# A hybrid Fourier and neighbourhood-attention block on one core: the two passes over the MLP's weights are parted, one put beside the queries, one beside the values, and the context's norm is made in steps

## The chip, the core and the metric

One core of a Trainium2 chip runs the whole program: TensorE (PE in the profile; PEld is its weight load), VectorE (DVE), ScalarE (ACT), GpSimd (POOL), SyncE (SP, which here only issues transfers) and 16 DMA engines. The metric is the device time of one execution in microseconds, the lower the better.

## What is computed

One layer, one batch, 2048 latent tokens of 1024 channels and 256 context tokens. What matters for the change, cut from the reference:

```
sh1, sc1, g1, sh2, sc2, g2 = ada_mod(c, w_ada, b_ada)       # silu(c) @ w_ada + b_ada, six times 1024
csh1, csc1, ...            = ada_mod(c_ctx, w_ada, b_ada)
hc = modulate(rms_norm(ctx, norm1_g), csh1, csc1)           # context: only keys and values are used
fc, qc, kc, vc = split_projection(hc @ w_in)
hx = modulate(rms_norm(x, norm1_g), sh1, sc1)
fx, qx, kx, vx = split_projection(hx @ w_in)                # 4 x 512 columns
...
gates = sigmoid(hx @ w_branch_gate)                         # 2048 columns
...
x   = x + g1 * mixed
hx2 = modulate(rms_norm(x, norm2_g), sh2, sc2)
x   = x + g2 * (relu(hx2 @ w_mlp1) ** 2) @ w_mlp2
```

## The kernel before, in words

The program is one stream of Python calls that a scheduler orders engine by engine; at run time every engine works through its own list in that order, and an instruction whose operand is missing holds what stands behind it on its engine. SP issues nearly all transfers, and its list too is in order: a load that waits for its buffer holds every store behind it.

**Input stage.** `run_pair(n)` goes through eight pairs of 256-column weight units (`seq`, line 689): two Fourier units; two gate units; a query unit with a gate unit (twice); two value units; a key unit with a gate unit (twice); two gate units. Matrix products are three float16 products (high and low halves, `mm3`, line 76), into four PSUM tiles of 2 KB per partition (`mmp`, 4 buffers) that all kinds of units share. A gate or Fourier unit makes 128 channels x 512 tokens with 24 matmuls of 512 columns, which ACT evicts (`put_T`, line 516, tile `ot`, 2 buffers) and SP stores. A query or key unit makes 128 tokens x 256 columns with 24 matmuls of 256 columns: ACT squares it (`sq`, line 572), DVE sums and scales, POOL takes the power (`rstd_from`, line 171), DVE normalises (`qn`, 577), turns (585 to 588), and three units later PE transposes the result (`tq`, 603), and ACT and DVE split it (`sH`, `sL`). A value unit is evicted by ACT (`vo`, line 646, 2 buffers), DVE takes its largest value (648), SP stores it.

I name the pairs by their place: the **gates** (pair 1), the **first queries** and the **second queries** (pairs 2 and 3, each 16 query units and 8 gate units), the **values** (pair 4: 36 units, context's four among them).

**Side work.** Beside the units runs a generator, `side_work` (line 294). `tick` (line 440) moves it on after each unit: three steps per two units in the gates, one per unit in the queries and values. Its steps, in order: context's shift and scale (`c`: eight parts of two steps; a part is a load of 1 MB of `w_ada` into tile `awt`, 2 buffers, and a weighted sum on DVE, `ada_sum`, lines 274 to 277); the second norm's shift and scale (`m`, eight parts); the two residual gains (`g`, eight parts of two steps, with a small bias load `br`); the bias table of the attention (`wm`: three steps, each a load, a subtraction on POOL and a store to `tT`; lines 325 to 327); then 32 steps `w12m`, each a load of 1 MB of an MLP weight into the same two `awt` buffers. For the 16 parts of `w_mlp1` DVE takes the largest magnitude (line 338), for the 16 of `w_mlp2` ACT sums the squares (line 340). From both come the scales `msc`, with which the MLP's weights are then prepared (`early_blocks`, tiles `raw`, `wo`, `ws`), from the end of the side work on.

**Context's norm.** At the start of pair 3 the two context tiles are loaded and normalised (`load_x`), and `build` (line 223) makes the normalised, modulated, transposed and split `hc` in one go: for each of eight channel groups two transposes on PE (`tp_c`, line 229), a scale and shift on ACT or DVE in turn (`ht_c`, 235 or 233), the high half on ACT (236), the low half on DVE (237). `hc` is first used by the value units of context.

Of the kernel before, what the change touches and what calls it, by code (L numbers as in the profile page):

```python
# [8 lines left out]
F32 = mybir.dt.float32  # L9
F32R = mybir.dt.float32r  # L10
F16 = mybir.dt.float16
# [10 lines left out]
C = 256  # L22
# [41 lines left out]
def dit_block(ctx: ExitStack, tc: tile.TileContext, a, out, taps=None, upto=9):  # L64
# [125 lines left out]
    def load_x(src, r0, name, xh=None, sq_on_dve=False, scale_on_dve=False):  # L190
        if xh is None:
            xh = pb.tile([128, D], F32, tag="xh", name=f"xh_{name}", bufs=5)
        load(xh, src[r0:r0 + 128, :])
        sq = pb.tile([128, D], F32, tag="xsq", name=f"xsq_{name}")
        ss = pb.tile([128, 1], F32, tag="ss", name=f"ss_{name}", bufs=4)
        if sq_on_dve:
            dve.tensor_tensor_reduce(out=sq, in0=xh, in1=xh, op0=ALU.mult, op1=ALU.add, scale=1.0, scalar=0.0, accum_out=ss)
        else:
            act.activation(sq, xh, AF.Square, accum_out=ss)
        rs = rstd_from(pb, ss, 1, 1.0 / D, name)  # L200
        if scale_on_dve:
            dve.tensor_scalar(out=xh, in0=xh, scalar1=rs, scalar2=None, op0=ALU.mult)
        else:
            act.activation(xh, xh, AF.Copy, scale=rs)
        return xh
# [17 lines left out]
    def build(hx, xhs, ab, name):  # L223

        w = hx.shape[3]
        for k in range(KT):
            tp = tpp.tile([128, 512], F32, tag="tp", name=f"tp_{name}_{k}")[:, :w]
            for i, xh in enumerate(xhs):
                pe.transpose(tp[:, i * 128:(i + 1) * 128], xh[:, k * 128:(k + 1) * 128], ident)
            sc, bi = ab[:, 8 + k:9 + k], ab[:, k:k + 1]  # L230
            t = pb.tile([128, 512], F32, tag="ht", name=f"ht_{name}_{k}", bufs=2)[:, :w]
            if k % 2:
                dve.tensor_scalar(out=t, in0=tp, scalar1=sc, scalar2=bi, op0=ALU.mult, op1=ALU.add)
            else:
                act.activation(t, tp, AF.Identity, bias=bi, scale=sc)
            act.activation(hx[:, 0, k], t, AF.Copy)
            dve.tensor_tensor(out=hx[:, 1, k], in0=t, in1=hx[:, 0, k], op=ALU.subtract)
        return hx

    def power_of_two(dst, top, floor):  # L240

# [38 lines left out]
    def ada_cols(dst, j, c0, gain, name, acc, wt=None, nk=KT):  # L280

        ps = adp.tile([128, 512], F32, tag="ad", name=f"ad{name}")
        for i in range(2):
            bs = slice(i * 128, (i + 1) * 128)

            for k in range(nk, KT):
# [4 lines left out]
        dve.scalar_tensor_tensor(out=dst[:, 8 + j:9 + j], in0=dst[:, 8 + j:9 + j], scalar=1.0, in1=gain,  # L291
                                 op0=ALU.add, op1=ALU.mult)

    def side_work():
        for dst, d0, s0, g0, o in ((ABc, 0, 8, 16, "c"), (AB2, 3 * D, 0, 24, "m")):
            for k in range(KT):
                c0 = d0 + k * 128
                acc = ada_sum(ada_load(c0, c0 + D, f"{o}{k}"), s0, f"{o}{k}")
                yield
                ada_cols(dst, k, c0, vecT[:, g0 + k:g0 + k + 1], f"{o}{k}", acc)  # L300
                yield
            if o == "c":
                norm_scale(ABc, 1, "c")
                yield
# [17 lines left out]
        for ct in range(3):  # L322
# [3 lines left out]
            pool.tensor_tensor(t, t, view(r, 63 + (0, -8, -8)[ct], [[-1, 16], [1, w]]), op=ALU.subtract)  # L326
            sp.dma_start(tT[ct].rearrange("c d k -> d c k"), t)
            yield
        for i in range(32):
            wt = pb.tile([128, KT, 256], F32, tag="awt", name=f"w12m{i}", bufs=2).rearrange("p k n -> p (k n)")  # L330
            j = i % 16
            if i < 16:
                sp.dma_start(wt, a["w_mlp1"][0, j // 2 * 128:(j // 2 + 1) * 128, j % 2 * 2048:(j % 2 + 1) * 2048])
            else:
                sp.dma_start(wt.rearrange("p (k n) -> p k n", k=2),
                             a["w_mlp2"][0, j * 256:(j + 1) * 256, :].rearrange("(k p) n -> p k n", p=128))
            if i < 16:
                dve.tensor_reduce(out=w1m[:, j:j + 1], in_=wt, axis=AX.X, op=ALU.max, apply_absolute_value=True)
            else:
                act.activation(wt, wt, AF.Square, accum_out=w2m[:, j:j + 1])  # L340
            yield
        m = pb.tile([128, 10], F32, tag="msd", name="msd")
        for i, src in enumerate((w1m, AB2[:, 8:16], w2m, AB2[:, 0:8])):
            dve.tensor_reduce(out=m[:, i:i + 1], in_=src, axis=AX.X, op=ALU.max, apply_absolute_value=True)
# [542 lines left out]
    for n in range(len(seq)):  # L887
        if n == 1:
            with tc.issue_after(last_load[0].ins):
                load_gains()  # L890
                load_rope()
        if n == 3:
            xh_c = [load_x(a["ctx"][0], i * 128, f"c{i}") for i in range(2)]
            hx["c"] = build(pb.tile([128, 2, KT, C], F16, tag="hc", name="hc"), xh_c, ABc, "c")
        if n == len(seq) - 1:
            for o in beside + blocks[:1]:
                for _ in o:
                    pass
            turn(0)
            adp.release()  # L900
            tpp.release()
            pb.release()
            fb = sbuf("ffb")
            chp = psum("ffch", 3)
            smp = psum("ffsm", 1)
            chan = fb.tile([128, 392], F32, tag="chan", name="chan")
            sp.dma_start(chan, a["chan"])
            beside = [fourier_prep()]
        run_pair(n)
        if seq[n][0][0] == "v":  # L910
            beside.append(split_values())
# [952 lines left out]
```

## Time and profile before

| | us |
|---|---|
| median of three runs (lowest, highest) | 2658.93 (2656.83, 2659.85) |
| the profiled execution's own time | 2660.88 |
| its span, first to last instruction | 2659.1 |
| PE busy in the span | 2538.6 (95%) |
| DVE, ACT, POOL busy | 1827.3 (69%), 1183.3 (44%), 484.4 (18%) |
| mean granted TensorE clock | 0.985 |

The span is the time from the first to the last instruction on the core; 1.8 us of the execution's time lie around it. PE is busy through nearly all of it, so what PE loses is read stage by stage: its idle time, what it waited for, and how fast its matmuls ran just after. The gates run from 157 to 244 us, the first queries to 335, the second queries to 449, the values to 556.

### The profile page before, as it was taken

How to read it: one execution, taken by the hardware profiler on the slowest of the kernel's cores; microseconds unless marked ns; L12 is line 12 of the kernel's file. 1: busy time of each engine (PE TensorE's matmuls, PEld its weight loads, DVE VectorE, ACT ScalarE, POOL GpSimd, SP SyncE). 2: the span in 40 equal slices, each digit the busy share in tenths (PEclk: the TensorE clock that was granted, in tenths of full speed). 3: DMA queues.
4: the chain of work that ended last, by engine and by line, in shares of the span. 5: the costliest groups of instructions: out<-in, count | busy, mean ns of one | idle time of the engine just before them, and what ended most of it. 6: DMA issues, size and time to landing. Idle time of an engine off the chain costs nothing.

```text
span 2659.1 us, 42665 instructions
## 1 busy us (share of the span) xinstructions
PE 2538.6 (95%) x15830; PEld 1473.0 (55%) x15830; DVE 1827.3 (69%) x3672; ACT 1183.3 (44%) x2113; POOL 484.4 (18%) x715
## 2 busy tenths in 40 slices
PE   6899989898999899998999999999999999999999
PEld 5445756776656678875666444444444444444444
DVE  6756976568553678887777696978877644636367
ACT  5623225545242577874444564627351333314050
POOL 1201221012224545452000121121211100000000
PEclk9999999999999999998999999999999999999999
DMA  8577689867374744556767777787766533333334
GB/s 269 137 225 204 203 248 304 270 204 245 93 249 141 199 118 138 148 169 207 237 226 264 260 242 261 231 279 233 268 235 230 181 99 105 101 103 99 104 103 155
DMA packets 345962, 517.77 MB, mean 195 GB/s; under 512 B 48497, under 2 KB 210505, under 8 KB 341401
## 3 DMA queue, kind: packets, MB, share of 16 engines
q1 hardware_dynamic: 296425, 406.50, 48.8%
q0 software_dynamic: 29104, 75.23, 8.4%
q10 hardware_dynamic: 20224, 33.31, 3.9%
q8 instruction: 124, 2.03, 0.3%
q14 instruction: 85, 0.70, 0.1%
HBM read 370.11 MB, written 145.84 MB: 194 GB/s over the span
## 4 chain that ended last, share of the span: by engine, by line
PE 68%; DMA 11%; DVE 11%; issue 3%; ACT 3%; POOL 3%; SPq 2%; DVEq 0%; ACTq 0%; POOLq 0%
PE p L82 21%; PE pm L82 17%; PE ps_g L82 8%; PE po L82 6%; DMA w12m<-in_w_mlp 3%; PE pua L82 2%; PE ps_k L82 2%; PE tp L1325 2%; PE pmf L1263 2%; PE pv L1339 1%; SPq L188 1%; PE ps_f L82 1%; PE ps_v L82 1%; PE sc L1303 1%; DVE wo L387 1%
## 5 line engine op out<-in xcount | busy, mean ns | idle before, releaser
L82 PE MATMUL pm<-hc,wb 128*128 128x512 f16 x2688 | 582.6, 379 | 5.6 <-DVE p L1605 2.1
L82 PE MATMUL p<-wb,a 128*128 128x512 f16 x2688 | 581.9, 379 | 2.1 <-DVE X L1605 1.5
L82 PEld LDWEIGHTS <-wb 128*128 128x128 f16 x2688 | 262.9, 98 | 323.6 <-issue 7.3
L82 PEld LDWEIGHTS <-a 128*128 128x128 f16 x2688 | 263.0, 98 | 319.7 <-issue 2.9
L82 PE MATMUL ps_g<-hx,w_g 128*128 128x512 f16 x1536 | 342.5, 380 | 0.9 <-ACT ot_f L516 0.9
L1605 DVE TENSOR_TENSOR X<-X,p 128x512 f32<-128x512 f32 x280 | 184.5, 685 | 171.1 <-PE p L82 151.8
L82 PEld LDWEIGHTS <-hx 128*128 128x128 f16 x2304 | 227.4, 99 | 39.6 <-issue 7.2
L82 PEld LDWEIGHTS <-w_g 128*128 128x128 f16 x1536 | 151.0, 99 | 171.2 <-issue 3.2
L1091 POOL DMA_DIRECT2D bt<-tT x264 | 132.4, 508 | 76.3 <-DVE ri L1332 53.0
L1605 DVE TENSOR_TENSOR u<-pm,u 128x512 f32<-128x512 f32 x128 | 87.5, 690 | 84.3 <-PE pm L82 82.5
L1312 DVE CUSTOM_DVE_ANT_0 s<-sc,bt,qsc 128x736 f32<-128x736 f32 (+5 forms) x128 | 111.2, 869 | 37.1 <-PE sc L1306 33.9
L386 ACT ACTIVATE wo<-ws,msc 128x512 f16<-128x512 f32 x96 | 69.0, 718 | 152.0 <-DVE ws L430 124.0
L1609 ACT ACTIVATE p<-pm 128x512 f32<-128x512 f32 x32 | 18.9, 589 | 239.7 <-PE pm L82 239.7
L1739 POOL DMA_DIRECT2D xr<-x1d x32 | 17.3, 539 | 569.8 <-DVE X L1605 562.1
L1333 DVE SCALAR_TENSOR_TENSOR pL<-tp,pH 128x640 f16<-128x640 f32 (+1 forms) x128 | 112.3, 878 | 5.0 <-ACT pH L1328 4.5
L1316 ACT ACTIVATE s<-s,m 128x736 f32<-128x736 f32 (+5 forms) x128 | 104.6, 817 | 16.5 <-DVE m L1312 13.9
L386 ACT ACTIVATE wo<-raw,msc 128x512 f16<-128x512 f32 x128 | 87.4, 709 | 52.0 <-DVE raw L430 17.8
L82 PE MATMUL po<-wouH,mH 128*128 128x512 f16 x256 | 97.3, 384 | 9.3 <-DVE ga L1383 9.3
L1325 PE MATMUL tp<-ident,s 128*128 128x128 f32 x704 | 103.1, 281 | 0.8 <-ACT s L1316 0.7
L516 ACT ACTIVATE ot_g<-ps_g,usc_g 128x512 f32<-128x512 f32 x64 | 43.4, 681 | 130.9 <-PE ps_g L82 117.6
L82 PE MATMUL po<-wouL,mH 128*128 128x512 f16 x256 | 98.8, 386 | 2.4 <-POOL wouL L1536 2.4
L387 DVE SCALAR_TENSOR_TENSOR wo<-raw,msc,wo 128x512 f16<-128x512 f32 x128 | 94.4, 748 | 8.0 <-ACT wo L386 7.9
(535 smaller groups left out, 4645.9 us busy)
## 6 DMA issues: line engine op xcount, KB each, us to landing
wb<-w1d SPq DMA_DIRECT2D x224, 256.0 KB
wb<-w2d SPq DMA_DIRECT2D x224, 256.0 KB
w12m<-in_w_mlp SPq DMA_DIRECT2D x32, 1024.0 KB
raw<-in_w_mlp ACTq DMA_DIRECT2D x24, 1024.0 KB
w1d<-wo POOLq DMA_DIRECT2D x84, 256.0 KB, 4.0
w2d<-wo POOLq DMA_DIRECT2D x84, 256.0 KB, 4.0
gT<-ot_g SPq DMA_DIRECT2D x64, 256.0 KB
hc<-hcd SPq DMA_DIRECT2D x14, 1024.0 KB
```

The lines of the kernel that those rows point to most:

```text
L82: last_mm[0] = pe.matmul(ps, l, r, start=(start and i == 0), stop=(stop and i == n - 1))
L188: last_load[0] = sp.dma_start(dst, src)
L386: act.activation(hi, src, AF.Copy, scale=scale)
L387: dve.scalar_tensor_tensor(out=lo, in0=src, scalar=scale, in1=hi, op0=ALU.mult, op1=ALU.subtract)
L516: act.activation(o, ps, func, scale=scale)
L1091: load_(t[i * 16:(i + 1) * 16, :, off + j0 * w:off + (j0 + 8) * w], raw(tT[ct], (2 * hp * 15 + dr) * w, [[120 * w, 16], [15 * w, 2], [1, 8 ...
L1263: pe.matmul(ps, l, r, start=(i == 0), stop=(i == len(prods) - 1))
L1312: tail["dve"] = dve.tensor_tensor_reduce(out=s[:, :n], in0=sc, in1=bias, op0=ALU.add, op1=ALU.min, scale=qsc[:, 4:5], scalar=3.0e38, accum ...
L1316: tail["act"] = act.activation(s[:, :n], s[:, :n], AF.Exp, bias=m1[:, 0:1], scale=-1.0, accum_out=m1[:, 1:2])
L1325: tail["pe"] = pe.transpose(tp[:, i * 128:(i + 1) * 128], s[:, o:o + 128], ident)
L1333: tail["dve"] = dve.scalar_tensor_tensor(out=pL[:, :c], in0=tp[:, :c], scalar=PTOP, in1=pH[:, :c], op0=ALU.mult, op1=ALU.subtract)
L1605: last["dve"] = dve.tensor_tensor(out=o, in0=x, in1=y, op=op)
```

## The change

The 32 steps over the MLP's weights become a generator, `mlp_weights(which)`, that is called at two places: the 16 parts of `w_mlp2` (squares on ACT) after context's shift and scale, ahead of `m`; the 16 parts of `w_mlp1` (maxima on DVE) at the old place behind the bias table. What stands between them in the list of steps (`m`, `g`, the bias table) comes 16 steps later than before. Context's loads, norm and `build` are no longer called at the start of pair 3, but become a generator of ten steps, `context()`, that `tick` moves on beside the side work from there, with the transposes of a step placed behind the matmul issued last. No instruction is added or taken away among those that compute.

```
 def side_work():
     for dst, d0, s0, g0, o in ((ABc, 0, 8, 16, "c"), (AB2, 3 * D, 0, 24, "m")):
+        if o == "m":
+            yield from mlp_weights(range(16, 32))
         for k in range(KT):
 ...
-    for i in range(32):
-        wt = pb.tile([128, KT, 256], F32, tag="awt", name=f"w12m{i}", bufs=2).rearrange("p k n -> p (k n)")
 ...
-        yield
+    yield from mlp_weights(range(16))
+def context():
+    xh = []
+    for i in range(2):
+        xh.append(load_x(a["ctx"][0], i * 128, f"c{i}"))
+        yield
+    hx["c"] = pb.tile([128, 2, KT, C], F16, tag="hc", name="hc")
+    for k in range(KT):
+        with tc.issue_after(last_mm[0].ins):
+            build_k(hx["c"], xh, k, ABc, "c")
+        yield
 ...
     if n == 3:
-        xh_c = [load_x(a["ctx"][0], i * 128, f"c{i}") for i in range(2)]
-        hx["c"] = build(pb.tile([128, 2, KT, C], F16, tag="hc", name="hc"), xh_c, ABc, "c")
+        beside.append(context())
```

`build_k` is the body of `build`'s loop over k, unchanged, and `mlp_weights` has the body of the loop that it replaces.

**ACT's list at the gates**, from the ninth gate unit's eviction on (`ot_g` is an eviction, `w12m` a sum of squares, `w_q` the high half of the next query weights). Before:

```order
L516 ACTIVATE ot_g_0_1740<-ps_g_0_1715,usc_g_1198 128x512
L516 ACTIVATE ot_g_1_1781<-ps_g_1_1756,usc_g_1198 128x512
L516 ACTIVATE ot_g_0_1827<-ps_g_0_1802,usc_g_1202 128x512
L516 ACTIVATE ot_g_1_1860<-ps_g_1_1835,usc_g_1202 128x512
L516 ACTIVATE ot_g_0_1938<-ps_g_0_1913,usc_g_1198 128x512
L507 ACTIVATE w_q_1896<-ws_q_1535,usc_q_1707 128x1024 x2
```

Now, at the same unit (1740 is the ninth):

```order
L322 ACTIVATE w12m_1874,w2m<-w12m_1874 128x2048
L538 ACTIVATE ot_g_0_1740<-ps_g_0_1715,usc_g_1198 128x512
L322 ACTIVATE w12m_1931,w2m<-w12m_1931 128x2048
L322 ACTIVATE w12m_1962,w2m<-w12m_1962 128x2048
L538 ACTIVATE ot_g_1_1781<-ps_g_1_1756,usc_g_1198 128x512
L322 ACTIVATE w12m_1965,w2m<-w12m_1965 128x2048
L538 ACTIVATE ot_g_0_1827<-ps_g_0_1802,usc_g_1202 128x512
L322 ACTIVATE w12m_1996,w2m<-w12m_1996 128x2048
L322 ACTIVATE w12m_2027,w2m<-w12m_2027 128x2048
L538 ACTIVATE ot_g_1_1860<-ps_g_1_1835,usc_g_1202 128x512
```

The 16 squares stand between the eighth gate unit's eviction and that of the second gate unit of the first queries; the last five have query squares (`sq_q`) between them.

**DVE's list where the maxima stand** (`w1m<-w12m`; the other rows are steps of the query units, or `vmax`, the largest value of a value unit). Before, around the end of the first queries:

```order
L338 TENSOR_REDUCE w1m<-w12m_3702 128x1
L585 TENSOR_TENSOR t_q_3_3281<-qn_q_3_3278,rcos 128x256
L586 TENSOR_TENSOR t_q_3_3282<-qn_q_3_3278,rsin 128x256
L338 TENSOR_REDUCE w1m<-w12m_3760 128x1
L574 TENSOR_REDUCE ss_q_0_3447<-sq_q_0_3445 128x4
L588 TENSOR_TENSOR qr_q_3_3280<-t_q_3_3281,t_q_3_3282 128x8x16 x2
L574 TENSOR_REDUCE ss_q_1_3502<-sq_q_1_3500 128x4
L169 TENSOR_SCALAR ms_q_0_3449<-ss_q_0_3447,usc_q_2683 128x4
L233 TENSOR_SCALAR ht_c_3374<-tp_c_3371,ABc 128x256
L169 TENSOR_SCALAR ms_q_1_3504<-ss_q_1_3502,usc_q_2683 128x4
L338 TENSOR_REDUCE w1m<-w12m_3812 128x1
```

Now the first stands behind the eighth query unit of the second queries, and the last six among the values:

```order
L320 TENSOR_REDUCE w1m<-w12m_4811 128x1
L632 TENSOR_TENSOR sL_q_4525<-tq_q_2_4606,sH_q_4524 128x2x4x16
L670 TENSOR_REDUCE vmax<-vo_v_2_4679 128x1
L670 TENSOR_REDUCE vmax<-vo_v_3_4711 128x1
L632 TENSOR_TENSOR sL_q_4525<-tq_q_3_4613,sH_q_4524 128x2x4x16
L320 TENSOR_REDUCE w1m<-w12m_4843 128x1
L632 TENSOR_TENSOR sL_q_4525<-tq_q_3_4613,sH_q_4524 128x2x4x16
L670 TENSOR_REDUCE vmax<-vo_v_0_4743 128x1
L670 TENSOR_REDUCE vmax<-vo_v_1_4775 128x1
L320 TENSOR_REDUCE w1m<-w12m_4881 128x1
```

Before, the 16 maxima span nine query units and the 16 squares five more and eight values; now the maxima span eight query units and ten values.

## Rows read from the trace of the kernel before

**Rows 1.** Busy time by stage: gates, first queries, second queries, values. Columns: stretch and its length, then busy us and instructions of PE, PEld, DVE, ACT, POOL; granted clock; DMA engines' busy share; GB/s.

```profile
157.00:244.00 87.00, 86.38 (x427) 42.39 (x427) 41.15 (x129) 24.18 (x30) 2.43 (x3) 1.00 0.69 200
244.00:335.00 91.00, 91.00 (x643) 63.90 (x641) 83.70 (x280) 29.66 (x68) 20.54 (x18) 1.00 0.74 213
335.00:449.00 114.00, 96.44 (x639) 63.93 (x638) 87.66 (x197) 45.34 (x93) 22.40 (x22) 0.96 0.87 270
449.00:556.00 107.00, 98.49 (x878) 86.20 (x876) 52.94 (x126) 60.78 (x96) 2.98 (x5) 0.98 0.82 272
```

**Rows 2.** What PE waited for from 335 to 500 us: total us, times, longest us.

```profile
PE tq_q L603 <- DVE qr_q L588: 8.7, 4, 5.4
PE ps_v L82 <- ACT vo_v L646: 6.5, 4, 3.7
PE tq_q L603 <- DVE sL_q L610: 4.7, 3, 2.1
PE tp_c L229 <- ACT ht_c L235: 3.2, 2, 2.6
```

**Rows 3.** The maxima on DVE in the second queries, the squares on ACT there and in the values: busy us, mean ns | idle time of the engine just before them and what ended it.

```profile
L338 DVE TENSOR_REDUCE w1m<-w12m 128x1 f32<-128x2048 f32 x16 | 36.6, 2286 | 18.8 <-DMA w12m<-in_w_mlp 18.7
...
L340 ACT ACTIVATE w12m<-w12m 128x2048 f32<-128x2048 f32 x7 | 13.4, 1909 | 11.1 <-DMA w12m<-in_w_mlp 11.1
...
L340 ACT ACTIVATE w12m<-w12m 128x2048 f32<-128x2048 f32 x9 | 17.2, 1910 | 13.2 <-DMA w12m<-in_w_mlp 13.2
```

**Rows 4.** PE in order of time: start, us, instruction [idle before]. Three pieces, after a long wait in the second queries, without one, and after one in the values.

```profile
379.53 6.68 PE L82 MATMUL ps_g<-hx,w_g 128*128 128x512 f16 x24
...
386.27 5.40 PE L82 MATMUL ps_q<-w_q,hx 128*128 128x256 f16 x48
...
477.86 7.02 PE L82 MATMUL ps_v<-w_v,hx 128*128 128x256 f16 x48 [3.68 <-ACT vo_v L646]
```

**Rows 5.** Tile `w12m`, all its instructions: count, shortest/median/longest ns, start of the first and of the last.

```profile
L333 SPq DMA_DIRECT2D w12m<-in_w_mlp x16: 327/340/3822, 327.5 to 405.0; - x16
L338 DVE TENSOR_REDUCE w1m<-w12m x16: 2281/2286/2287, 335.0 to 413.3; 128x1 f32<-128x2048 f32 x16
L335 SPq DMA_DIRECT2D w12m<-in_w_mlp x16: 367/372/384, 409.4 to 480.3; - x16
L340 ACT ACTIVATE w12m<-w12m x16: 1903/1910/1912, 418.1 to 486.8; 128x2048 f32<-128x2048 f32 x16
```

**Rows 6.** The chain of work that ended last, from 405 to 490 us: start, us from issue to landing of a load of `w_mlp2`.

```profile
415.61 5.50 DMA w12m<-in_w_mlp
...
423.16 5.03 DMA w12m<-in_w_mlp
...
441.42 9.44 DMA w12m<-in_w_mlp
...
461.25 7.66 DMA w12m<-in_w_mlp
```

**Rows 7.** SP's issues at the gates, in order of time.

```profile
193.26 1.01 SPq L188 DMA_DIRECT2D awtc<-in_w_ada  x2
...
198.80 0.99 SPq L188 DMA_DIRECT2D awtm<-in_w_ada  x2
...
204.34 1.89 SPq L188 DMA_DIRECT2D awtm<-in_w_ada  x2
```

**Rows 8.** PE at the gates (the eighth gate unit, and later the first and second gate unit of the first queries).

```profile
195.46 5.34 PE L82 MATMUL ps_g<-hx,w_g 128*128 128x512 f16 x24
...
250.25 5.34 PE L82 MATMUL ps_g<-hx,w_g 128*128 128x512 f16 x24
...
261.61 5.34 PE L82 MATMUL ps_g<-hx,w_g 128*128 128x512 f16 x24
```

**Rows 9.** DVE in the second queries, in order of time: the third, fourth and eighth of the maxima, with the wait before each.

```profile
345.30 2.29 DVE L338 TENSOR_REDUCE w1m<-w12m 128x1 f32<-128x2048 f32 x1 [1.23 <-DMA w12m<-in_w_mlp]
...
351.79 2.29 DVE L338 TENSOR_REDUCE w1m<-w12m 128x1 f32<-128x2048 f32 x1 [2.01 <-DMA w12m<-in_w_mlp]
...
376.04 2.29 DVE L338 TENSOR_REDUCE w1m<-w12m 128x1 f32<-128x2048 f32 x1 [3.10 <-DMA w12m<-in_w_mlp]
```

**Rows 10.** SP in the second queries: a load and a store of the bias table, and the loads of `w_mlp1` between them.

```profile
338.94 0.36 SPq L325 DMA_DIRECT2D wm<-in_wmask  x1
343.42 3.31 SPq L333 DMA_DIRECT2D w12m<-in_w_mlp  x1
349.19 0.36 SPq L327 DMA_DIRECT2D tT<-wm  x1
```

**Rows 11.** DVE, one part of a residual gain's sum (in the first queries), in order of time.

```profile
302.04 0.61 DVE L274 TENSOR_SCALAR aaccg<-awtg,sil 128x256 f32<-128x256 f32 x2
302.57 2.46 DVE L276 SCALAR_TENSOR_TENSOR aaccg<-awtg,sil,aaccg 128x256 f32<-128x256 f32 x6
...
305.27 0.42 DVE L277 TENSOR_TENSOR aaccg<-aaccg 128x256 f32<-128x256 f32 x1
...
305.93 0.41 DVE L311 TENSOR_TENSOR aaccg<-aaccg,br 1x256 f32<-1x256 f32 x1
```

More of the change, by code (lines that the diff above doesn't have):

```diff
@@ L226, in build, with build_k @@
         for k in range(KT):
[L227 to L237, printed above, removed]
-        return hx
+            build_k(hx, xhs, k, ab, name)
+        return hx
+    def build_k(hx, xhs, k, ab, name):
+        w = hx.shape[3]
+        tp = tpp.tile([128, 512], F32, tag="tp", name=f"tp_{name}_{k}")[:, :w]
+        for i, xh in enumerate(xhs):
+            pe.transpose(tp[:, i * 128:(i + 1) * 128], xh[:, k * 128:(k + 1) * 128], ident)
+        sc, bi = ab[:, 8 + k:9 + k], ab[:, k:k + 1]
+        t = pb.tile([128, 512], F32, tag="ht", name=f"ht_{name}_{k}", bufs=2)[:, :w]
+        if k % 2:
+            dve.tensor_scalar(out=t, in0=tp, scalar1=sc, scalar2=bi, op0=ALU.mult, op1=ALU.add)
+        else:
+            act.activation(t, tp, AF.Identity, bias=bi, scale=sc)
+        act.activation(hx[:, 0, k], t, AF.Copy)
+        dve.tensor_tensor(out=hx[:, 1, k], in0=t, in1=hx[:, 0, k], op=ALU.subtract)
+    def context():
[8 more added lines that the diff above has]
+            yield
     def power_of_two(dst, top, floor):
@@ L292, in ada_cols, with mlp_weights @@
                                  op0=ALU.add, op1=ALU.mult)
+    def mlp_weights(which):
+        for i in which:
+            wt = pb.tile([128, KT, 256], F32, tag="awt", name=f"w12m{i}", bufs=2).rearrange("p k n -> p (k n)")
+            j = i % 16
+            if i < 16:
+                sp.dma_start(wt, a["w_mlp1"][0, j // 2 * 128:(j // 2 + 1) * 128, j % 2 * 2048:(j % 2 + 1) * 2048])
+            else:
+                sp.dma_start(wt.rearrange("p (k n) -> p k n", k=2),
+                             a["w_mlp2"][0, j * 256:(j + 1) * 256, :].rearrange("(k p) n -> p k n", p=128))
+            if i < 16:
+                dve.tensor_reduce(out=w1m[:, j:j + 1], in_=wt, axis=AX.X, op=ALU.max, apply_absolute_value=True)
+            else:
+                act.activation(wt, wt, AF.Square, accum_out=w2m[:, j:j + 1])
+            yield
     def side_work():
         for dst, d0, s0, g0, o in ((ABc, 0, 8, 16, "c"), (AB2, 3 * D, 0, 24, "m")):
+            if o == "m":
+                yield from mlp_weights(range(16, 32))
             for k in range(KT):
@@ L328, in side_work @@
             yield
-        for i in range(32):
-            wt = pb.tile([128, KT, 256], F32, tag="awt", name=f"w12m{i}", bufs=2).rearrange("p k n -> p (k n)")
[L331 to L340, printed above, removed]
-            yield
+        yield from mlp_weights(range(16))
         m = pb.tile([128, 10], F32, tag="msd", name="msd")
```

## The prediction

> **What bounds the kernel now.** I read the busy times first. PE is busy for 95% of the span, so a change is worth what it gives back of PE's idle time or of its slow matmuls. By stage [rows 1], the gates and the first queries leave PE almost nothing idle (87.0 - 86.4 and 91.0 - 91.0 us), while the second queries leave 114.0 - 96.4 = 17.6 us and the values 107.0 - 98.5 = 8.5 us: 26.1 us together.
>
> Next, PE's waits there [rows 2]: for DVE's turned and split queries (8.7 and 4.7 us), for ACT's eviction of values (6.5) and for context's `ht_c` (3.2). Neither engine is full at that moment. What ended their own idle time are the loads of the MLP's weights: DVE sat 18.8 us ahead of its maxima, ACT 11.1 and 13.2 us ahead of its squares [rows 3]. A maximum that waits for its 1 MB stands in DVE's list ahead of query steps, and PE stops once it has run through its free banks.
>
> The loads come as fast as two buffers and the shared DMA engines allow: the 16 maxima start 413.3 - 335.0 = 78.3 us apart, 5.22 us each; the 16 squares 68.7 us, 4.58 us each [rows 5]. The list asks for more. All 32 stand between the 15th query unit and the eighth value. Take 24 matmuls of a gate as 5.3 us and of a query or value as 2.7 us [rows 4, 8]: 17 queries, 8.5 gates and 8 values are 46 + 45 + 22 = 113 us, 3.5 us each. That is the stall's origin: a stretch with 32 MB of side loads, beside stages with half as many.
>
> PE pays a second time: the 24 matmuls after the longest wait took 6.68 us where 5.34 is usual, and 48 after the value wait 7.02 where 5.40 is usual [rows 4, 8]. That is 3.0 us at the lower clock level (mean granted clock 0.96 and 0.98 in these stages, 1.00 before them [rows 1]).
>
> **What the change moves, and what each part costs.**
>
> *The 16 squares, to the gates.* Removed from the second queries and values; no work is added, as ACT is busy 24 of 87 us at the gates [rows 1] and gets 12 to 13 squares of 2.1 us. The question is whether their loads arrive. The first takes the buffer and the place of an `m` load that is issued at 198.8 us, the second that at 204.3 [rows 7]; a load takes 5.0 to 5.5 us in the quieter part of today's stretch and up to 9.4 in the crowded part [rows 6], so the first square can start at 204.3. The last must come before the eviction of the second gate of the first queries, which PE ends at 261.6 + 5.3 = 266.9 [rows 8]; PE can then go through three more banks, two queries and a gate, 10.7 us, to 277.6. At today's spacing of the squares, 4.58 us, the last ends at 204.3 + 15 x 4.58 + 2.1 = 275.1: in time. At the maxima's 5.22 it ends at 284.7: 7.1 us of stall. I take 1 us, since the gates hold fewer other transfers than today's place (DMA busy 0.69 there, 0.82 to 0.87 here [rows 1]); bounds 0 and 7.1. Behind each waiting square stand gate evictions, and behind these their stores on SP; the new query weights' high halves stand behind the seventh and ninth square, due 10 us before PE needs them.
>
> The Trainium skill, "DMA: Bandwidth & Descriptors", section "Anatomy of one DMA", gives a transfer about 2.0 us plus its bytes over 436 GB/s, for the other kind of queue; my estimate from it is 4.4 us for 1 MB, under the least in [rows 6]. By it this stall would be 0; the range keeps the rows' bounds.
>
> *`m` and `g`, 16 steps later.* The same DVE sums; the first queries get fewer (PE has no idle time there with more), the second queries get seven or so parts of `g`.
>
> *The 16 maxima, now from the eighth query unit of the second queries to the tenth value.* PE's time over that is 8 x 2.9 (with the transposes) + 4 x 5.3 + 10 x 2.7 = 71 us, 4.8 us each, against 3.2 before (nine queries, 4.5 gates). At 5.22 us the last is 7 us late, less than the 10.7 us that PE can go on. But the eight loads beside the bias table come slower: from 335.0 to 376.04, 5.9 us each [rows 5, 9], as a store of the table waits on POOL and the next loads wait behind it on SP (343.4 to 349.2 [rows 10]). The table moves along with the maxima, so this remains: eight maxima now stand over five queries and 2.5 gates, 27 us, take 41, so are 14 us late, 3.5 us more than PE can bridge. DVE adds to it. A part of `g` is 0.61 + 2.46 + 0.42 + 0.41 = 3.9 us [rows 11]; seven are 27, less six maxima (13.7) that leave for the values: DVE's 87.7 us in the second queries [rows 1] become 101 where PE needs some 93. Part of the maxima's waits now holds DVE work behind it that before was done elsewhere; I add 2.5 us, about a third of that excess. Together 6 us; bounds 0 (at the squares' spacing) and 17.6 (all that this stage loses today).
>
> *Context in ten steps.* The same instructions, spread over ten units; PE waited 3.2 us for `ht_c` among the maxima [rows 2], which now stand later. I take 1; bounds 0 and 3.2. Its two loads also leave SP's list ahead of Fourier stores, at no cost to PE either way.
>
> *The values.* They lose nine squares and get six maxima, for which 4.8 us each are given; DVE has room (52.9 of 107 [rows 1]). I take 1 us of the 8.5; bounds 0 and 8.5.
>
> *The clock.* With a third of the waits left, 1 of 3.0 us; bounds 0 and 3.0.
>
> **The sum.** Taken away: 17.6 + 8.5 + 3.0 = 29.1 us. Coming back: 1 + 6 + 1 + 1 + 1 = 10 us. Gain 19 us on the profiled execution's 2660.9, which was 2.0 above the median of the runs: 2641.8 by the profile, **2640 us** by the median. With all costs at their lower bounds 2630; with all at the upper (39.4) 2669.
>
> **The rivals.**
>
> *The second queries keep their stall.* They hold the bias table, seven parts of `g`, context's steps and ten maxima on a DVE that would be asked for 101 of 93 us. For it: the sums above. Against it: the first queries ran without a wait with DVE at 83.7 of 91 us [rows 1], and DVE's excess can run over into the values. If 14 us stay there rather than 6, with 1 us more at the values and 2 of clock, 19 us come back and 10 are gained: 2649.
>
> *The gates stall, and it is slower.* A square that waits for its load holds every eviction behind it. The place is the gates' last eight units and the first six of the first queries; the stall there is 204.3 + 15 s + 2.1 - 277.6, or 15 s - 71.2 us, for a spacing s. The trace's slowest run of loads is 5.9 us [rows 9], which gives 17; with the other 9 us that costs 26 of 29. The point from which it decides is 6.1 us (20.1 us of stall, no gain). At 6.5 us, that is with 2 x 6.5 - 2.1 = 10.9 us from issue to landing, the stall is 26.3, 6 us more than the gain: 2665. Against it: no small packets stand beside these loads, and the gates' DMA share is the lowest of the four. The Trainium skill, "Perfetto Trace Analysis", section "Per-engine timelines", calls ACT and DVE strict first-in-first-out, which is this rival's mechanism; by that rule nothing can pass a late square, and the trace agrees (a value eviction behind a late square, then PE's 3.68 us wait [rows 4]).
>
> *No change.* The bytes are the same, and the DMA engines are busy 0.69, 0.74, 0.87 and 0.82 of the four stages [rows 1], 314 of 399 us. If transfers set the pace of the whole, the waits only go to other stages, and 25 to 30 us come back: 2655 to 2660, 2658 in the middle. Against it: 85 us of slack, over half of it at the gates and first queries.
>
> That the change doesn't do what it says is excluded by the lists: loads, squares and maxima stand where it puts them.
>
> **How the numbers follow.** Forecast (2632 to 2648): 0.62. Second queries keep their stall (2646 to 2654, middle 2649): 0.20. Gates stall and slower: 0.08. No change: 0.10. Two tenths may lie outside: I leave out the slower rival and most of no change and go from 2630, the bound of the sum, to 2655. A measurement of this kernel tells about 0.2% from no change, 5.3 us: faster means under 2653.6. All of the forecast and nearly all of the first rival are, with 0.01 of the rest: 0.82. Within 0.2%: 0.10; slower: 0.08.
>
> **What would show it.** Right: PE busy all but a few us in the second queries and values, which together take some 202 us instead of 221; ACT's wait ahead of the squares halved, no PE wait on `ot_g` over 3 us at the gates; a spacing of the squares under 4.9 us. Wrong step by step: a PE wait for `qr_q` or `sL_q` over 10 us in the second queries (first rival); a wait of `ps_g` or `ps_q` on ACT between 230 and 290 us, with a spacing over 5 us (second); the same idle total spread over all four stages (third). What I would be most wrong about is the spacing of the squares' loads, which no row shows at the gates.

## The result: slightly slower, and the profile after

| | before | after |
|---|---|---|
| median of the runs on the same chips, us | 2664.92 (8 runs) | 2670.34 (8 runs) |
| ratio after / before, 95% interval | | 1.0028 [1.0016, 1.0041] |
| the profiled execution's time, us | 2660.88 | 2672.78 |

The forecast was 2640 us, a gain; the kernel came out 0.28% slower. The five runs of the kernel before that were added beside it lie at 2664 to 2669, so the loss is some 7 us by the ratio, not the 12 between the two profiled executions.

The stages of the kernel after, in the columns of [rows 1] (gates, first queries, second queries, values):

```profile
157.00:244.00 87.00, 87.00 (x428) 42.23 (x426) 28.97 (x94) 37.03 (x43) 1.43 (x2) 1.00 0.73 232
244.00:335.00 91.00, 84.87 (x598) 58.95 (x597) 60.08 (x203) 39.48 (x72) 18.01 (x17) 0.98 0.75 234
335.00:449.00 114.00, 103.06 (x686) 69.01 (x684) 97.56 (x282) 33.83 (x89) 26.25 (x21) 0.97 0.73 214
449.00:556.00 107.00, 96.61 (x815) 82.41 (x815) 76.66 (x153) 44.24 (x81) 5.87 (x7) 0.94 0.80 264
```

PE's idle time in the second queries fell from 17.6 to 10.9 us, but the first queries, which had none, lose 6.1, the values lose 10.4 instead of 8.5, and the granted clock is lower there (0.98 for 1.00, 0.94 for 0.98). Where PE stands says when: first value matmul at 448.76 before and 452.84 after, first key 555.94 and 563.42. So 7.5 us are lost by the first key. Little of it is idle time: from 157 to 556 us PE idles 27.5 us after and 26.7 before. What grew are the matmuls that run slowly behind a wait: 10.5 us in the events below, where the prediction found 3.0 before.

Four events hold 21 of the 27.5 us of idle time and these slow matmuls. **One**, in the first queries (ACT, DVE and PE in order of time; the number in brackets is the wait before an instruction):

```profile
272.86 1.91 ACT L322 ACTIVATE w12m<-w12m 128x2048 f32<-128x2048 f32 x1 [1.23 <-DMA w12m<-in_w_mlp]
...
282.63 0.62 DVE L289 TENSOR_SCALAR aaccm<-awtm,sil 128x256 f32<-128x256 f32 x2 [2.44 <-DMA awtm<-in_w_ada]
...
283.72 0.41 PE L625 MATMUL tq_q<-ident,qr_q 128*128 128x128 f32 x2 [2.28 <-DVE sL_q L632]
286.07 4.16 PE L82 MATMUL ps_q<-w_q,hx 128*128 128x256 f16 x24 [1.94 <-DVE qn_q L599]
```

The last square ends at 274.8, as forecast (275.1), and the loads of `m` behind it are as late as it is: DVE waits for the second one with query steps behind it. With four shorter waits PE loses 6.1 us here, and 24 matmuls take 4.16 us instead of 2.78.

**Two**, the longest, at the end of `g` in the second queries (SP, POOL, DVE, PE):

```profile
382.13 0.24 SPq L344 DMA_DIRECT2D br<-in_b_ada  x1
...
388.32 1.00 SPq L188 DMA_DIRECT2D awtg<-in_w_ada  x2
389.13 0.41 DVE L345 TENSOR_TENSOR aaccg<-aaccg,br 1x256 f32<-1x256 f32 x1
389.38 0.91 SPq L350 DMA_DIRECT2D wfr<-in_w_fourier_out  x1
390.39 1.52 SPq L344 DMA_DIRECT2D br<-in_b_ada  x1
392.02 0.34 SPq L354 DMA_DIRECT2D rp<-in_rpb  x1
...
404.72 0.41 DVE L345 TENSOR_TENSOR aaccg<-aaccg,br 1x256 f32<-1x256 f32 x1 [7.15 <-DMA br<-in_b_ada]
404.89 1.06 POOL L355 TENSOR_SCALAR rp<-rp,qsc 120x128 f32<-120x128 f32 x1 [11.37 <-DMA rp<-in_rpb]
...
405.81 0.66 PE L625 MATMUL tq_q<-ident,qr_q 128*128 128x128 f32 x2 [6.20 <-DVE sL_q L632]
406.27 8.08 PE L82 MATMUL ps_g<-hx,w_g 128*128 128x512 f16 x24
```

`wfr` is a copy from memory to memory, 252 rows of 4 KB, that the attention needs at 900 us. Behind it stands `br`, a bias of 1 KB, which is there 14.3 us after its issue began; DVE waits 7.15 us for it, POOL 11.4 us for `rp`, a load of 15 KB. The load of `br` before it, with a load of `g` ahead of it and no copy, was there within 7.0 us, and nothing waited (382.13 to 389.13). PE loses 6.2 us, and 2.7 more by 24 matmuls at 8.08 instead of 5.34: behind the wait the granted clock is at the lower of its two levels (0.50, 1.2 GHz):

```profile
405.80:409.00 3.20, 3.19 (x9) 1.47 (x10) 2.82 (x10) 0.72 (x3) 1.28 (x2) 0.50 0.21 87
```

In the kernel before, the copy stood at the end of the Fourier stage. There too `rp` was there only 13.1 us after its issue, but PE lost nothing by it (from 141 to 250 us it waited once, 0.9 us, for an eviction by ACT):

```profile
141.14 0.78 SPq L316 DMA_DIRECT2D wfr<-in_w_fourier_out  x1
142.03 0.47 SPq L320 DMA_DIRECT2D rp<-in_rpb  x1
...
155.08 0.61 POOL L321 TENSOR_SCALAR rp<-rp,qsc 120x128 f32<-120x128 f32 x1 [21.31 <-DMA rp<-in_rpb]
```

The code of the copy and its place in `side_work` are untouched. Side work is ordered behind the load issued last when `tick` is called; in the kernel before, that was context's second load, taken early (140.75), and the copy, emitted in the same tick, went early with it. Now it is a load of `g`.

**Three**, at the first value: POOL waits 10.2 us for a part of the bias table, a query's power stands behind that, and PE behind this (2.92 us, and 4.39 instead of 2.78). **Four**, the end of the side work, where `pms` and `pmb` stand in PE's list among the values:

```profile
450.41 0.95 POOL L360 TENSOR_TENSOR wm<-wm,rp 120x384 f32<-120x384 f32 x1 [10.18 <-DMA wm<-in_wmask]
451.31 1.02 POOL L171 TENSOR_TENSOR rs_q<-ms_q,mhalf 128x4 f32<-128x4 f32 x1
...
452.84 4.39 PE L82 MATMUL ps_v<-w_v,hx 128*128 128x256 f16 x24 [2.92 <-DVE qn_q L599]
...
495.85 0.27 PE L369 MATMUL pms<-ident,msd 128*4 128x128 f32 x1 [2.51 <-DVE msd L366]
495.95 5.10 PE L82 MATMUL ps_v<-w_v,hx 128*128 128x256 f16 x30
504.27 0.59 PE L374 MATMUL pmb<-msd,ones 4*128 4x4 f32 x2 [3.21 <-DVE msd L371]
504.79 4.02 PE L82 MATMUL ps_v<-w_v,hx 128*128 128x256 f16 x18
508.61 6.47 PE L82 MATMUL ps_v0c<-w_v,hc 128*128 128x256 f16 x48
```

5.7 us of waits; at 5.40 us for 48 matmuls, the 96 that follow would take 10.8 us and take 15.6. Together the four events are 7.5 + 8.9 + 4.5 + 10.5 = 31 us, about what the forecast took away (29.1).

### The profile page after: what moved, and what is told of

Read it like the earlier page. It is cut to its first block, busy times and chain, and to the rows that moved or that the text cites. A ratio compares the mean times of both kernels' runs of the same rounds, so it can differ in the third digit from the quotient of the medians.

```text
span 2671.0 us, 42655 instructions
## 1 busy us (share of the span) xinstructions
PE 2548.9 (95%) x15830; PEld 1479.5 (55%) x15830; DVE 1824.3 (68%) x3672; ACT 1181.6 (44%) x2113; POOL 487.8 (18%) x715
## 4 chain that ended last, share of the span: by engine, by line
PE 69%; DMA 11%; DVE 11%; ACT 3%; POOL 3%; issue 3%; SPq 1%; DVEq 0%; POOLq 0%; ACTq 0%
PE p L82 21%; PE pm L82 18%; PE ps_g L82 7%; PE po L82 6%; PE pua L82 3%; DMA w12m<-in_w_mlp 2%; PE tp L1346 2%; PE ps_k L82 2%; PE ps_f L82 2%; PE pmf L1284 2%; PE pv L1360 2%; DMA raw<-in_w_mlp 1%; PE sc L1324 1%; DVE wo L409 1%; DMA wm<-in_wmask 1%
## 5 line engine op out<-in xcount | busy, mean ns | idle before, releaser
L82 PE MATMUL po<-wouH,mL 128*128 128x512 f16 x256 | 98.8, 387 | 0.0
```

The source lines that it names most:

```text
L82: last_mm[0] = pe.matmul(ps, l, r, start=(start and i == 0), stop=(stop and i == n - 1))
```

## The experiments

Ratios are to the kernel before (medians 2660.7 to 2662.8 in these sessions), with 95% intervals. All times are medians.

| run | what stands in it | us | ratio |
|---|---|---|---|
| e3_context_only | context in steps | 2666.64 | 1.0028 [1.0016, 1.0040] |
| e2_split_only | passes parted | 2675.53 | 1.0059 [1.0043, 1.0075] |
| e15_copy_late | copy late | 2666.15 | 1.0019 [1.0009, 1.0030] |
| e6_context_clean | context in steps, copy early | 2653.13 | 0.9971 [0.9958, 0.9984] |
| e5_split_clean | passes parted, copy early | 2666.57 | 1.0014 [1.0003, 1.0026] |
| e1_wfr_early | both, copy early | 2657.25 | 0.9987 [0.9974, 0.9999] |
| e4_wfr_end | both, copy early, later end | 2651.08 | 0.9962 [0.9947, 0.9976] |

**The copy early, in the changed kernel.**

```
 def side_work():
+    sp.dma_start(wfr, ...)            # and rp's memset and load
     for dst, d0, s0, g0, o in ...
-    sp.dma_start(wfr, ...)            # behind the gains
```

> The changed kernel with one copy moved: the 1 MB copy of the Fourier weights to wfr, and the small load rp behind it, are issued before the side work instead of behind the residual gains. Theory (a late small load): in the changed kernel the copy stands on SP between a gain's load and the 1 KB bias load br; br lands 14 us after its issue, DVE waits 7.2 us for it, PE 6.2 us, and the next 24 matmuls take 8.08 us instead of 5.34. Without it these 8.9 us come back: 2670.3 - 8.9 = 2661 us, and no wait of PE over 3 us between 396 and 410 us. Rival (transfers set the pace of the whole): the wait goes to another place, 2668 to 2671. Rival (DVE is over-asked in the second queries, 97.6 of 114 us): PE goes on waiting there for sL_q and qr_q, at least 4 of the 6.2 us remain, 2666 or more.

Measured 2657.25: by the ratios 0.41% less than the changed kernel, 11 us (some 6 to 16 by the two intervals, so the 8.9 us of the rows lie within). PE runs from 395 to 412 us without a wait, and the first key is at 551.76 instead of 563.42. The late loads behind the copy are shown as a cause. The rivals are out.

**Each part alone, and the same with the copy early.** Against the changed kernel:

```
 e2
-            beside.append(context())
+            xh_c = [load_x(a["ctx"][0], i * 128, f"c{i}") for i in range(2)]
+            hx["c"] = build(..., xh_c, ABc, "c")
 e3
-            if o == "m":
-                yield from mlp_weights(range(16, 32))
...
-        yield from mlp_weights(range(16))
+        yield from mlp_weights(range(32))
 e5 is e2, and e6 is e3, with the copy early as above
```

> The changed kernel with context's loads, norm and build in one go at the start of the second queries, as before: the parting of the two passes alone. Theory (four separate events: squares ahead of query steps 7.5 us, late br 8.9, POOL held by the bias table 4.5, end of the side work 10.5): none of them hangs on context's steps, since the copy wfr stands between a gain's load and br here too; PE's waits for ht_c are 2.4 us in steps and were 3.2 + 0.6 in one go: 2670 to 2673. Rival (context in steps is what made it slower): 2660 or less.

> The kernel before with context in ten steps, nothing else: the 32 MLP parts stand together as before. Theory (late small load): here too the copy wfr moves from 141 us to the place between two bias loads br, at the start of the second queries, so DVE waits for a br some 5 to 9 us and PE with it; context's waits of 3.8 us mostly go: 2664.9 + 7 - 3 = 2669, between 2665 and 2672. Rival (steps help and the copy costs nothing): 2661 or less.

> The parting of the two passes alone, with the copy wfr and the load rp issued before the side work. Theory (the copy is a cost of its own that comes with either part of the change): in the run of the parting alone POOL waited 13.7 us for rp behind the copy, PE 5.6 us for qn_q, and the next 24 matmuls took 4.9 us instead of 2.8: these 7.7 us come back, 2675.5 - 7.7 = 2668 us (2665 to 2670). Rival (the copy matters only where br is held): 2674 or more.

> The kernel before with context in ten steps and the copy issued before the side work. Theory: the copy's price goes (in the run of context's steps alone PE waited 4.7 us for an eviction at the end of the first queries), and so do context's waits in one go, 3.8 us: 2666.6 - 4.7 = 2662 less some of 3.8, so 2659 to 2662, a little under the kernel before (2662.8). Rival (steps cost what they save): 2662 to 2664.

The parting alone is 0.59% slower, 2.5 us over the first range; context alone 0.28%, within its range. In both the copy goes late too, since in both the copy's tick no longer follows context's early loads: so each needs to be judged with the copy early. Then context in steps **gains 0.29%, 7.7 us**, and the parting **costs 0.14%, 4 us**. The first is 6 us more than expected, the second within its range. They add up: -0.29 + 0.14 is -0.15, and both together gave -0.13. The copy costs 0.57% beside context's steps, 0.45% beside the parting, 0.41% with both. How it does differs. In the run of the parting alone nobody waits for `br`; POOL waits for `rp`, with the powers of the queries behind it:

```profile
405.01 0.61 POOL L355 TENSOR_SCALAR rp<-rp,qsc 120x128 f32<-120x128 f32 x1 [13.70 <-DMA rp<-in_rpb]
...
410.34 4.91 PE L82 MATMUL ps_q<-w_q,hx 128*128 128x256 f16 x24 [5.62 <-DVE qn_q L599]
```

In that of context's steps alone it is ACT that waits, for a context tile, with a gate's eviction behind it. The two context tiles, of 512 KB each, stand on SP on either side of the copy (316.23): the first is there 5.9 us after its issue, the second after 14.5:

```profile
315.44 0.38 SPq L188 DMA_DIRECT2D xh_c<-in_ctx  x1
317.74 0.38 SPq L188 DMA_DIRECT2D xh_c<-in_ctx  x1
...
321.31 1.06 ACT L199 ACTIVATE xsq_c<-xh_c 128x1024 f32<-128x1024 f32 x1 [3.00 <-DMA xh_c<-in_ctx]
332.19 1.06 ACT L199 ACTIVATE xsq_c<-xh_c 128x1024 f32<-128x1024 f32 x1 [5.85 <-DMA xh_c<-in_ctx]
...
333.97 2.90 PE L82 MATMUL ps_g<-hx,w_g 128*128 128x512 f16 x7 [4.68 <-ACT ot_g L536]
```

**The copy late, in the kernel before.** Against the kernel before (`rp`'s load is put behind the same load):

```
     def ada_load(c0, c1, name, wt=None):
...
+        side_load[0] = last_load[0]
         return wt
...
+        with tc.issue_after(side_load[0].ins):
             sp.dma_start(wfr, ...)
```

> The kernel before, with the copy of the Fourier weights and the small load rp held behind a gain's load, so that they are issued at about 330 us, between bias loads br, and not at 141; nothing else. Theory (the copy is a cost by itself: what is issued behind it lands some 14 us later, and DVE, POOL or ACT waits with the query steps behind it): 2662 + 8 to 11 = 2670 to 2673 us. Rival (it costs only where the other parts of the change have put the maxima or context's steps): 2661 to 2665.

0.19%, 5 us (2.4 to 8.0 by the interval): less than my range, at or over the rival's. The copy and `rp` issued late are a cost by themselves:

```profile
314.91 0.78 SPq L320 DMA_DIRECT2D wfr<-in_w_fourier_out  x1
...
316.49 0.33 SPq L325 DMA_DIRECT2D rp<-in_rpb  x1
...
328.86 0.61 POOL L326 TENSOR_SCALAR rp<-rp,qsc 120x128 f32<-120x128 f32 x1 [8.09 <-DMA rp<-in_rpb]
```

Beside context's steps the cost is larger (0.57%); with the 0.41 and 0.45% of the other two the intervals overlap. In every run `rp` moves with the copy, so what `rp` alone would cost late was not tested; the bias load above came late with the copy and no `rp` ahead of it.

**The end of the side work later.** Against e1_wfr_early, at `pms` and again at `pmb`:

```
-        yield
+        for _ in range(3):
+            yield
         ps = adp.tile([128, 512], F32, tag="ad", name="pms")
```

> As the first, and the two matmuls at the end of the side work (pms, pmb) are issued two steps later each, so that PE's list holds 48 and 120 more value matmuls ahead of them. Theory: in the changed kernel PE waits 2.5 and 3.2 us for msd there and runs its next 96 matmuls at about half speed for a while (15.6 us instead of 10.8); both come back but for 1 or 2 us: 2661 - 9 = 2652 us. Rival (transfers set the pace; the wait moves to raw, the loads of the MLP's preparation, or to eviction): within 2 us of the first.

0.25% less than without it, 6 to 7 us of the 9 expected; the waits for `msd` are gone, and the first key is at 546.27. So far it looked as if the parting had made this loss, with the maxima last. The next two runs speak against that. Against e1_wfr_early, eight squares stay at the gates and eight go behind the maxima; the second run has the later end with it:

```
-                yield from mlp_weights(range(16, 32))
+                yield from mlp_weights(range(16, 24))
...
-        yield from mlp_weights(range(16))
+        yield from mlp_weights((*range(16), *range(24, 32)))
```

> The changed kernel with the copy early, and only eight of the 16 squares at the gates; the other eight stand behind the maxima again, at the side work's end. Theory (two places of loss that the parting made: 16 squares reach into the first queries, 4.8 us of waits and 1.4 of slow matmuls there; and the maxima at the end leave DVE's msd late, 5.5 us of waits and some 4 of slow matmuls): with eight squares the last starts near 240 us, before the queries, and the end waits for ACT alone: 2657 - 6 - 8 = 2643, less some us that come back in the second queries, where the maxima stand eight steps earlier: 2645 us (2642 to 2650). Rival (the waits for these loads only move): about what context in steps gives without any parting, 2653 us or more.

> The same with the two matmuls at the side work's end issued two steps later each. Theory: with squares last, msd comes early on DVE as in the kernel before (0.7 us of wait), so that the delay gives nothing: within 1.5 us of the last. Rival (the end is a cost in any order): 4 to 6 us less than the last.

2659.17 (0.9991 [0.998, 1.0001]) and 2652.3 (0.9964 [0.9951, 0.9977]). Half the squares are no better than all of them: the first queries are mended (1.7 us of waits), and the second queries are worse, as the maxima start 34 us sooner, at 366.6 instead of 400.6:

```profile
244.00:335.00 91.00, 89.26 (x637) 62.70 (x635) 78.11 (x260) 31.04 (x66) 18.62 (x18) 1.00 0.74 220
335.00:449.00 114.00, 99.67 (x666) 66.71 (x664) 96.98 (x231) 32.87 (x83) 30.80 (x21) 0.99 0.80 247
```

And PE does not wait for `msd` there, yet the later end gives 7 us:

```profile
484.37 0.27 PE L369 MATMUL pms<-ident,msd 128*4 128x128 f32 x1
```

The two gains do not lie in the same place, as far as one profiled execution of each can tell. With all squares at the gates the later end brings the first key 5.5 us forward (551.76 to 546.27). With half of them the first key comes 2.0 us later (552.5 to 554.5), and the first matmul of the MLP 9.9 us sooner (1479.0 to 1469.1): there the gain is made behind the keys' start.

I then held it for a price of the MLP's preparation that follows, in any order of the passes:

> The kernel before with context in ten steps, the copy early, and the two matmuls at the side work's end (with the preparation of the MLP's weights behind them) two steps later each; the passes not parted. Theory now (the later end pays because the preparation's loads and DVE steps come later, whatever the order of the passes): 2653 - 6 = 2647 us, the lowest of all. Rival (only a list with the maxima last needs it): 2652 to 2655.

> The kernel before with nothing but the later end. Theory now: 2662 - 6 = 2656 us. Rival (only a list with the maxima last needs it): 2660 to 2663.

2650.57 (0.9960 [0.9944, 0.9975]), 0.11% under context in steps with the copy early, which by the intervals can be nothing or the 6 us expected; and 2659.58 (0.9999 [0.9985, 1.0013]), no gain in the kernel before, where 2656 is outside the interval. So the theory fell too, as one for any order. Shown is that the waits for `msd` go with a later end; why it pays where nothing waited for it stays open.

**Less waiting for the passes' loads.** Six edits of e4_wfr_end (2651.08): the bias table behind the maxima; squares spread between the parts of `m` and maxima between those of `g`; the squares on loads of 128 KB, or the maxima (these two kernels leave the rest of those weights out); squares spread between the parts of `c`, without and with the table at the gates.

```
e7   yield from mlp_weights(range(16))   # now ahead of the table's loop
e8   yield from mlp_weights((16 + 2 * k,))       # behind each of m's two steps; maxima in g's likewise
e9   sp.dma_start(wt[:, 0:256], ...)             # squares over wt[:, 0:256], seven times
e10  sp.dma_start(wt[:, 0:256], ...)             # maxima over wt[:, 0:256], eight times
e11  yield from mlp_weights((16 + 2 * k,))       # as e8, in c's parts
e12  next(tab)                                   # e11 with the table in c's third, fifth and seventh part
```

> The kernel with the copy early and the side work's end later, and the bias table behind the maxima, among the values, instead of ahead of them. Theory (POOL is held): the table's subtraction waits 7 to 11 us for its mask on POOL, the power of a query's scale (rs_q) waits behind it, and PE's waits for qn_q (2.4 and 2.0 us, and 1.6 for 24 slow matmuls) come from that; they go, and at the values POOL has nothing that PE waits for: 2651 - 5 = 2646 us. Rival (maxima and their loads set the second queries): the maxima stand three steps earlier, the stall stays, 2650 to 2653.

> As the last but one kernel before it in cause: copy early, end of side work later, and the 16 squares spread between the parts of m, the 16 maxima between the parts of g, so that three 1 MB loads fall to four steps everywhere instead of four to four and then two to four; the bias table comes last. Theory (the stalls come where loads stand closer than they arrive, 4.5 to 5.6 us each): four steps take 14 to 15 us of PE at the gates and queries, so 4.8 us are given per load; PE's idle time from 157 to 556 us, 16 us with these two mends alone, falls to 5 or less, and its slow matmuls with it: 2651 - 10 = 2641 us (2638 to 2645). Rival (transfers set the pace of the whole): 2649 to 2653.

> The kernel with the copy early and the side work's end later, but each square reads 128 x 256 elements of the second MLP weights seven times over in place of 128 x 2048 (128 KB loaded, not 1 MB; the sums are not those of the reference). ACT's time for a square stays near 1.7 us. Theory (the squares' loads, 4.6 us apart where the steps are 3.6 us, hold ACT and with it query squares; the first loads of m come late behind them): PE's 4.8 us of waits in the first queries and the half-speed matmuls after them (1.7 us) go: 2651 - 6 = 2645 us. Rival (ACT's order alone: 2 us squares ahead of evictions): the waits stay, 2650 to 2652.

> The same kernel with the maxima's loads cut from 1 MB to 128 KB instead (each maximum goes over 256 elements eight times, so that DVE's time is kept; not the reference's maxima). Theory (loads set the second queries and values): PE's waits for qn_q and sL_q from 400 to 470 us (2.4, 2.0, 2.2 us, with 2.3 us of slow matmuls) go: 2651 - 8 = 2643 us. Rival (DVE is over-asked there, 102 us of work in 114): the waits in the second queries stay, 2649 or more.

> The same kernel with all loads whole, and the squares spread between the parts of context's shift and scale (a load, a square, a square in turn, from the start of the side work), in the same 33 steps. Theory (a load per 4.8 us of PE at the gates where loads come 4.5 us apart): the waits of the first queries (4.8 us and 1.7 of slow matmuls) go: 2651 - 6 = 2645. Rival (squares wait for their loads among Fourier and gate evictions): PE waits for ot_f or ot_g instead, 2650 or more.

> The last, with the bias table's loads, subtractions and stores in the third, fifth and seventh part of context's shift and scale, where POOL has 1 us of work in 87; its three steps ahead of the maxima stay, empty. Theory (POOL held by the table's late masks, so that rs_q and qn_q come late): PE's waits for qn_q at 422 and 445 us (4.4 us and 2.3 of slow matmuls) go: 2645 - 6 = 2639 us. Rival (the maxima's own loads make these waits): 2644 to 2646.

Measured 2654.54, 2662.68, 2649.97, 2658.83, 2666.16 and 2664.87. None gave what I expected: the first and the third are as fast as e4_wfr_end within the noise, the other four 0.2 to 0.6% slower by the ratios. Each shows waits at another step. With the table last PE waits 5.9 us for the values' evictions. Even loads put squares among the query sums of the first queries, where PE is busy 77.9 of 91 us. With small squares PE still waits in the first queries (in the profiled execution, one of 2660.0 us): the order, made from modelled durations, now brings `m` forward on DVE, and its loads are late instead:

```profile
257.91 0.62 DVE L289 TENSOR_SCALAR aaccm<-awtm,sil 128x256 f32<-128x256 f32 x2 [3.26 <-DMA awtm<-in_w_ada]
...
264.01 5.30 PE L82 MATMUL ps_q<-w_q,hx 128*128 128x256 f16 x24 [5.06 <-DVE qn_q L601]
```

With small maxima DVE waits as long for them as with whole ones (12.7 and 11.3 us from 395 to 480), so their bytes do not make it. SP's list has their issues behind the table's stores, which wait for POOL, and behind the table's next loads; that this makes the wait is my reading:

```profile
SPq L362 <- POOL wm L361: 13.4, 3, 5.0
...
440.41 2.29 DVE L320 TENSOR_REDUCE w1m<-w12m 128x8 f32<-128x2048 f32 x1 [5.59 <-DMA w12m<-in_w_mlp]
...
448.98 0.66 PE L628 MATMUL tq_q<-ident,qr_q 128*128 128x128 f32 x2 [7.24 <-DVE qr_q L613]
```

With squares in `c`'s parts, the query weights' high half comes late behind them on ACT, and a matmul of `c` that shares a bank with the weights' scales holds PE for 11 us (7.3 us with the table there too):

```profile
245.32 1.01 PE L303 MATMUL adc<-ones,aaccc 128*128 128x1 f32 x4 [11.14 <-DVE usc_g L521]
```

## Why the prediction was wrong

**The step that failed first** is "*Context in ten steps*", with "Its two loads also leave SP's list ahead of Fourier stores, at no cost to PE either way". What left with them costs: the copy's place hung on them. The parting moves the copy too (e2_split_only), as the copy's step then comes 16 steps later, behind loads of `g`; "*`m` and `g`, 16 steps later*" counts DVE's sums and not what else stands there. I followed the instructions that the change writes elsewhere, and not those that only stood behind one of these. The prediction gives the copy no price. It is 0.41% in the changed kernel, 11 us, and turns a gain of 3.5 (0.3 to 6.9 by the interval) into a loss of 7.

**The gain was mis-sized as well.** *The 16 maxima* and *the values* were to leave 6 and 1 us of 26. With the copy early and context in steps, the parting takes PE's idle time in the second queries from 10.8 to 7.4 us and leaves the values as they were (7.9 and 7.8 us idle), and brings 4.8 to the first queries. Stages of both kernels, first without the parting (e6_context_clean), then with it (e1_wfr_early):

```profile
244.00:335.00 91.00, 91.00 (x644) 63.92 (x642) 81.20 (x270) 28.89 (x66) 19.56 (x18) 1.00 0.74 212
335.00:449.00 114.00, 103.22 (x688) 68.29 (x687) 94.91 (x222) 47.82 (x99) 23.25 (x24) 0.99 0.92 296
449.00:556.00 107.00, 99.11 (x883) 86.72 (x880) 52.76 (x126) 59.33 (x99) 1.70 (x4) 0.98 0.81 271
```

```profile
244.00:335.00 91.00, 86.22 (x601) 59.67 (x600) 62.68 (x205) 42.87 (x79) 16.84 (x17) 0.98 0.80 253
335.00:449.00 114.00, 106.57 (x715) 72.53 (x713) 100.77 (x293) 36.25 (x90) 28.12 (x24) 0.97 0.76 226
449.00:556.00 107.00, 99.17 (x885) 87.19 (x885) 73.65 (x146) 44.87 (x84) 2.48 (x5) 0.98 0.81 271
```

The first key is at 552.60 and 551.76: the parting is worth 0.8 us by then. What it costs lies behind that: in these two executions the last key matmul starts at 743.8 and 744.7 and the first of the MLP at 1474.3 and 1478.8, so some 1.7 us are lost in the keys and 3.6 between; what made them was not traced. "No change" was the right rival for this part, with another reason: not the transfers set the pace, since 14 MB less of them gave nothing (e10_small_maxima), but, as I read these runs, whichever step stands in an engine's list ahead of its operand. One sum of the rivals is off: the terms of *the second queries keep their stall* come to 20 us and not 19, so its middle is 2650; no chance hangs on that.

***The clock* was a term of the wrong size.** It was given 1 us, with 3.0 at most. The slow matmuls of the four events come to 1.4 + 2.7 + 1.6 + 4.8 = 10.5 us in the kernel after, more than the upper bound, while PE's idle time over the four stages hardly changed (26.7 and 27.5 us). The prediction took the slow matmuls as a share of the waits that are left; four waits of 1.9 to 3.2 us and one of 6.2 each had their own behind them.

**Where the mechanism was right and a size off.** The squares' spacing was 4.51 us ((272.9 - 205.3) / 15; forecast 4.58 or 5.22) and their end within 0.3 us; the cost of "*the 16 squares, to the gates*" was 7.5 us and not 1, just above the bound. I had PE go on until its banks were used up, and left out that the stream stays late: `m`'s loads, next in the same two buffers, hold DVE at 282.6, 8 us after the last square. The second rival had the right place and sign, but its spacing of 6.1 us never came. "*A part of `g`*" and DVE's excess in the second queries were right as work (97.6 us, 101 forecast); what PE waited for there was a load, not DVE's work.

**Right for a reason too small.** Context in steps was given 2 of 3.2 us. Alone, with the copy early, it gives 7.7. PE's waits for `ht_c` hardly change (3.2 us in [rows 2], 2.8 in e6_context_clean), those for `sL_q` grow from 4.7 to 7.0, but those for `qr_q`, 8.7 us, are gone. That `build`'s instructions in one piece among the maxima made these is my reading; no run tests it by itself.

**The base.** The three runs of before lay at 2657 to 2660; later ones of the same kernel at 2650 to 2672. A gain of 0.2% can be told only by runs on the same chip.

## What to carry to other kernels

Compare the whole lists of the queues, not only the rows that the change writes: an instruction whose place hangs on a moved one (here by "behind the last load") moves with it, and a large copy ahead of a 1 KB load is worth a look wherever it lands. A step that waits for a load and stands ahead of the critical chain on an in-order engine costs by its lateness, and taking one away brings up the next; price the stream that follows the moved work, not the moved work alone. When a change has several parts, run each alone with the side effects held fixed: here a gain of 8, a loss of 4 and a loss of 11 stood behind one number.

## What the runs showed of the hardware that was not expected

A 1 KB load issued 1.0 us behind a copy from memory to memory of 1 MB was there after 14.3 us, and a load of 15 KB behind that kept POOL waiting for 11.4. The Trainium skill, "DMA: Bandwidth & Descriptors", section "Queues, rings and completion order", says that each DMA engine takes descriptors in ring order and that a completion signal lands only after that engine's earlier writes; the rows of event two are in line with it, in that the two small loads, issued 1.6 us apart, were there within 0.2 us of each other; when the copy itself had landed no row shows. Without the copy ahead a load of `br` was there within 7.0 us, and of two context tiles the one ahead of the copy took 5.9 us and the one behind it 14.5. Loads of 128 KB were waited for as long as those of 1 MB (12.7 and 11.3 us in 85). And 24 matmuls after a wait of 6.2 us took 8.08 us, 1.5 times the usual 5.34; after 2.9 us 4.39, 1.6 times 2.78: the granted clock was 0.50 just behind the first of these waits, and 0.94 on the mean of the values, where the single waits were 3.2 us at most.
